# How many projection matmuls stand ahead of two blocks of a hybrid attention and delta-rule kernel

## The chip, the cores and the metric

The kernel runs on one core of one Trainium2 chip. The metric is device time in microseconds (us). The time before is the median of three runs.

## The reference

One transformer block on 1024 tokens of width 1024, in float32. A conditioning vector gives shifts, scales and gates. The normed input goes through one wide projection into nine parts: q, k and v of eight attention heads, q, k, v and z of eight heads of a gated delta rule, and two small logits. The attention is a sum of three dilated windows, which comes down to one biased softmax over 1024 keys. The delta rule works in chunks; within a chunk it solves a unit triangular system, and between chunks it carries a state. Both results go through an output projection, and a gated feed-forward layer follows.

```python
proj = h @ w_in[l]
q_a, k_a, v_a, q_d, k_d, v_d, z_d, b_d, a_d = jnp.split(proj, split_points, axis=-1)
y_attn = _dilated_attention(...)            # 8 heads of 64
y_delta = _gated_deltanet(...)              # 8 heads of 64, chunks, triangular solve, scan over chunks
y = jnp.concatenate([y_attn, y_delta], axis=-1) @ w_out[l]
x = x + g1 * y
h = _rmsnorm(x, norm_ffn_g[l]) * (1.0 + sc2) + sh2
y = (jax.nn.silu(h @ w_gate[l]) * (h @ w_up[l])) @ w_down[l]
```

## The kernel before, in words

The eight delta heads go in two groups of four (`delta(0)`, `delta(1)`). For each group the kernel convolves and transposes k and q, forms the products within chunks of 128 tokens (`delta_prep`), and inverts the triangular matrices (`delta_inverse`). The inverse has two parts. The diagonal 32x32 blocks are inverted on VectorE by 31 rounds of two instructions (lines 862 and 866), written to a DRAM scratch (`tn_d`, line 869) and read back in another layout (`tn`, line 871). Then the levels join the blocks into 64 and 128 by small matmuls on TensorE (tiles `lv`, `lw`, `lx`, lines 894 to 931), with copies on ScalarE and VectorE between them; the four heads go through them interleaved, `SKEW` = 4 steps apart. After the levels `delta_scan` walks over the eight chunks in order (tiles `st`, `o`, `yt`).

The large projections that nobody needs at once are a stock. The generator `others()` yields them step by step, in this order: z of the first delta group, then k, q and v of the second, z of the second (`z1`), the attention values in two halves (`va`, tile `g_va`), and q and k of the four head pairs (tile `g_a`), k first. A step is three matmuls, since each operand is split into a high and a low part: 128 columns by 256 for z and values (`proj_t`, counted as 0.32), by 512 for the others (`proj_d`, counted as 0.64). The generator `mixed()` adds the modulation matmuls (`mods`) after every 1.9 counted units, except while `quiet[0]` is set.

Three things draw on the stock. `turn(name)` draws `FILL[name]` counted units and then orders the matmuls of its block behind the last drawn one. `hold(what, us)` draws until `what` is complete, then `us` more, and orders the first matmuls of the levels behind the last drawn one; its arguments come from `LEVELS`, one pair for each group. And `until(...)` and `run(...)` draw what is left at certain places: all of z, values and pair 0's q and k before the attention, and the rest after the first pair's attention.

```python
LEVELS = ("qd", 4), ("z1", 28)
...
with hold(*LEVELS[g]) if step == 0 else ExitStack():
...
with turn(f"S{h}_{qb}_{c0}"):       # scores of head h, query block qb, keys from c0
```

The numbers are lower bounds on the order, not the order itself: the scheduler sorts instructions by priority and by when it reckons them ready, and so it places more of the stock between dependent matmuls (in the levels, in the scan, ahead of the first score) than these numbers ask for. At run time each engine takes its queue in the order that this gives.

The attention (`attend`) starts with `att_load(0)`: the head's q and k come back from DRAM (`raw`, two buffers), ScalarE makes QS and KS of them, GpSimd the low part KL (line 1227), and `att_score` multiplies QS with KS (line 1252) and with KL (line 1253). Its first block is `S0_0_0`. The first transposes have `et0_0_0` (1.92) and the first value product `y0_0` (0.64) as draws of their own.

Of the kernel before, what the change touches and what calls it, by code (L numbers as in the profile page):

```python
# [27 lines left out]
TCB = 3  # L28
MODS = 1.9
EARLY = 1  # L30
LEVELS = ("qd", 4), ("z1", 28)
TAIL = 4
AHEADF = 2
XB, ETB, AT, AV = 5, 4, 1, 3
# [13 lines left out]
    "et7_5_4": 0.64,  # L48
    "et2_7_0": 0.64,
    "et7_7_0": 0.64,  # L50
    "S0_0_0": 3.84,
    "et0_0_0": 1.92,
    "sy1_6": 1.92,
    "kk1_3_0_k": 0.64,
# [15 lines left out]
def build(tc, I, out):  # L70
# [772 lines left out]
    def delta_inverse(g, st):  # L843
# [92 lines left out]
        for step in range(3 * SKEW + 8):  # L936
            if step % SKEW == 0 and step // SKEW < 4:
                heads.append(head(step // SKEW))
            with hold(*LEVELS[g]) if step == 0 else ExitStack():
                quiet[0] = True  # L940
# [195 lines left out]
    def hold(what, us):  # L1136

        until(lambda: what in done)
        while us > 0:
            us -= next(fill[0])  # L1140
        return tc.issue_after(last[0].ins)
# [740 lines left out]
```

## Time and profile before

| | |
|---|---|
| median of three runs | 1458.61 us (1457.56 to 1468.36) |
| span of the profiled execution | 1472.9 us, 24559 instructions |
| mean granted TensorE clock in it | 0.964 |
| busy: PE, DVE, ACT, POOL | 95%, 59%, 45%, 19% of the span |
| longest lines of the chain that ended last | feed-forward matmuls (line 1513) and down projection (line 1699) |

The span is that of one execution under the profiler, from its first to its last instruction; the page gives no other time for this execution. It is longer than any of the three timed runs. The times of the parts below are those of the profiled execution.

PE is TensorE, PEld its weight loads, DVE VectorE, ACT ScalarE, POOL GpSimd, SP the engine that issues the transfers. The granted clock of PE is given as a fraction of its full rate; in this execution it is 1.00 or 0.50, and it changes at multiples of 3.41 us.

### The profile page before, as it was taken

Reading aid. Unit: us, or ns where it says so; the run is one execution under the profiler, and the core shown is the slowest. Engines: PE = TensorE matmul, PEld = TensorE weight load, DVE = VectorE, ACT = ScalarE, POOL = GpSimd, SP = SyncE. Lnnn points to the kernel's source line nnn. Section 1 sums busy time; section 2 is a strip of 40 time slices with the busy share of each in tenths; the row PEclk is TensorE's granted clock in tenths of the full one; section 3 lists DMA queues with packets and bytes.
Section 4 is the critical chain, followed back from the end, with each engine's and each line's share of the span. In section 5 each row is a group of like instructions: output and inputs, shape, how many; then the busy total and the mean of one; then the engine's idle time right before and its main releaser. Section 6 shows DMA issues by size and latency. Waiting matters only on the chain.

```text
span 1472.9 us, 24559 instructions
## 1 busy us (share of the span) xinstructions
PE 1400.0 (95%) x8984; PEld 1140.2 (77%) x8984; DVE 872.2 (59%) x1676; ACT 667.2 (45%) x1279; POOL 287.0 (19%) x267
## 2 busy tenths in 40 slices
PE   7998999988999989999999979999999999999997
PEld 4777767877889868777777758888888888888886
DVE  3687843565733332276525896766666676565477
ACT  3488414248122244476526733333333333445446
POOL 1344512244302332544235000000000000000000
PEclk9998999899957999999999989999999999999999
DMA  8736573475511535743165534454444565866666
GB/s 306 247 108 173 151 221 113 134 218 147 170 46 44 154 104 142 203 129 116 51 220 187 158 122 142 164 160 161 152 157 152 158 217 178 277 206 209 196 219 236
DMA packets 171345, 244.64 MB, mean 166 GB/s; under 512 B 33014, under 2 KB 76327, under 8 KB 171224
## 3 DMA queue, kind: packets, MB, share of 16 engines
q1 hardware_dynamic: 171224, 243.07, 52.7%
q8 instruction: 71, 1.16, 0.3%
q14 instruction: 50, 0.41, 0.1%
HBM read 180.25 MB, written 67.48 MB: 168 GB/s over the span
## 4 chain that ended last, share of the span: by engine, by line
PE 62%; DVE 7%; DMA 5%; ACT 2%; issue 2%; POOL 1%; SPq 0%; ACTq 0%; DVEq 0%
PE wga L1513 8%; PE wua L1513 8%; PE X L1699 6%; PE g_a L567 5%; PE wuc L1513 4%; PE wgc L1513 4%; PE Z L1699 4%; PE wo L567 4%; PE y L1293 3%; PE tr L1276 2%; PE Y L1699 2%; PE g_va L590 2%; PE wub L1513 2%; PE wgb L1513 2%; PE S L1252 1%
## 5 line engine op out<-in xcount | busy, mean ns | idle before, releaser
L1503 DVE TENSOR_TENSOR wl_db<-wr_db,wh_db 128x512 fp32r<-128x512 f32 x77 | 53.2, 691 | 76.1 <-ACT wh_db L1502 75.7
L1502 ACT CAST wh_db<-wr_db 128x512 fp32r<-128x512 f32 x77 | 47.9, 622 | 98.3 <-PE X L1699 41.3
L1699 PE MATMUL X<-wl_db,wh_da 128*128 128x512 f32 x176 | 68.6, 390 | 0.1
L1699 PE MATMUL X<-wh_db,wl_da 128*128 128x512 f32 x176 | 68.5, 389 | 0.0
L1699 PE MATMUL X<-wh_db,wh_da 128*128 128x512 f32 x176 | 68.5, 389 | 0.0
L1263 POOL TENSOR_SCALAR X<-X,sc 128x128 f32<-128x128 f32 (+7 forms) x64 | 47.7, 750 | 67.7 <-DVE sc L1262 55.1
L1261 ACT ACTIVATE X<-X,sc 128x128 f32<-128x128 f32 (+7 forms) x64 | 49.5, 775 | 23.8 <-DVE sc L1256 18.1
L1256 DVE CUSTOM_DVE_ANT_0 X<-S,ng 128x512 f32<-128x512 f32 (+3 forms) x64 | 36.8, 586 | 33.8 <-PE S L1253 21.7
L1222 DVE SCALAR_TENSOR_TENSOR QS<-raw,QS 64x1024 fp32r<-64x1024 f32 x8 | 12.6, 1572 | 70.3 <-ACT QS L1221 70.3
L567 PE MATMUL wo<-yh,wh_wo 128*128 128x512 f32 x128 | 52.0, 408 | 2.1 <-DVE xo L1339 1.0
L1503 DVE TENSOR_TENSOR wl_da<-wr_da,wh_da 128x512 fp32r<-128x512 f32 x77 | 52.6, 685 | 1.2 <-ACT wh_da L1502 1.2
L567 PE MATMUL g_a<-hh,wh_a 128*128 128x512 f32 x128 | 50.6, 395 | 0.0
L567 PE MATMUL g_a<-hh,wl_a 128*128 128x512 f32 x128 | 50.5, 395 | 0.0
L567 PE MATMUL wo<-yh,wl_wo 128*128 128x512 f32 x128 | 50.5, 396 | 0.0
L567 PE MATMUL g_a<-hl,wh_a 128*128 128x512 f32 x128 | 50.2, 392 | 0.0
L567 PE MATMUL wo<-yl,wh_wo 128*128 128x512 f32 x128 | 50.2, 394 | 0.0
L1502 ACT CAST wh_da<-wr_da 128x512 fp32r<-128x512 f32 x77 | 47.3, 616 | 5.8 <-PE wua L1513 5.8
L1293 PE MATMUL y<-et,va 128*64 128x128 f32 x576 | 46.0, 280 | 1.8 <-ACT et L1281 1.8
L1502 ACT CAST wh_wg_s<-wg_s 128x512 fp32r<-128x512 f32 x33 | 20.5, 622 | 58.0 <-PE wuc L1513 22.6
L1276 PE MATMUL tr<-ident,X 128*128 128x128 f32 x288 | 44.5, 280 | 2.2 <-ACT et L1281 2.0
L216 POOL TENSOR_TENSOR wl_wo<-wr_wo,wh_wo 128x512 fp32r<-128x512 f32 x24 | 32.8, 1366 | 57.4 <-ACT wh_wo L215 50.7
L1293 PEld LDWEIGHTS y<-et,va 128*64 128x64 f32 x576 | 33.7, 136 | 12.8 <-issue 8.7
(530 smaller groups left out, 4429.8 us busy)
## 6 DMA issues: line engine op xcount, KB each, us to landing
wr_da<-ao_d SPq DMA_DIRECT2D x77, 256.0 KB, 2.9
wm<-in_wada SPq DMA_DIRECT2D x64, 256.0 KB, 3.5
wr_wg<-in_wg SPq DMA_DIRECT2D x48, 256.0 KB, 3.0
wr_wu<-in_wu SPq DMA_DIRECT2D x48, 256.0 KB, 2.7
ao_d<-a SPq DMA_DIRECT2D x44, 256.0 KB, 2.2
wr_wd<-in_wdn SPq DMA_DIRECT2D x44, 256.0 KB, 3.1
wr_db<-wt_d SPq DMA_DIRECT2D x44, 256.0 KB, 2.7
ao_d<-as SPq DMA_DIRECT2D x33, 256.0 KB, 2.0
```

The source lines that it names most:

```text
L216: (eng or nc.gpsimd).tensor_tensor(out=lo[:, :n], in0=raw[:, :n], in1=hi[:, :n].bitcast(F32), op=ALU.subtract)
L567: last[0] = nc.tensor.matmul(ps, a[:, w0], b[k0 + k4][:, cs], start=(i == 0), stop=(i == n - 1))
L590: last[0] = nc.tensor.matmul(ps[:, :n], a[k][:, ts_], b[:, w0], start=(i == 0), stop=(i == 23))
L1256: nc.vector.tensor_tensor_reduce(out=X[:, c0:c1], in0=ps[:, 0 : c1 - c0], in1=ng[:, u + c0 : u + c1], scale=1.0, scalar=(3e38 if m is None ...
L1261: nc.scalar.activation(X[:, 0:nk], X[:, 0:nk], AF.Exp, scale=-1.0, bias=m, accum_out=sc[:, 2:3])
L1263: nc.gpsimd.tensor_scalar(out=X[:, 0:nk], in0=X[:, 0:nk], scalar1=sc[:, 3:4], scalar2=0.0, op0=ALU.mult, op1=ALU.add)
L1276: nc.tensor.transpose(ps[:, (kb - c0) * P : (kb - c0 + 1) * P], X[:, kb * P : kb * P + P], ident)
L1293: nc.tensor.matmul(yps[64 * e : 64 * e + 64, yc], va[:, kb, 64 * e : 64 * e + 64], ets[e][:, kb, :], start=(kb == 0), stop=(kb == qb),)
L1502: nc.scalar.copy(hi, src)
L1503: (eng or nc.vector).tensor_tensor(out=lo, in0=src, in1=hi.bitcast(F32), op=ALU.subtract)
L1513: nc.tensor.matmul(ps, a[:, w0], b, start=(first and k == 0 and n_ == 0), stop=(k == 3 and n_ == 2), skip_group_check=True,)
L1699: nc.tensor.matmul(bank[b], a[:, ts_], w, start=(first and f == 0 and n_ == 0), stop=(f == NF - 1 and n_ == 2), skip_group_check=True,)
```

## The change

Two numbers change. The second group's levels start after 36 counted units of value projections instead of 28, and the first attention score after 14.08 counted units of q and k projections instead of 3.84. The work itself is the same; the later draws find less of the stock left.

```diff
-LEVELS = ("qd", 4), ("z1", 28)
+LEVELS = ("qd", 4), ("z1", 36)
...
-    "S0_0_0": 3.84,
+    "S0_0_0": 14.08,
```

## The prediction

> **What bounds the kernel now.** I read the page first: who is busy, the granted clock by slice, the chain.
>
> ```profile
> PE 1400.0 (95%) x8984; PEld 1140.2 (77%) x8984; DVE 872.2 (59%) x1676; ACT 667.2 (45%) x1279; POOL 287.0 (19%) x267
> PEclk9998999899957999999999989999999999999999
> PE 62%; DVE 7%; DMA 5%; ACT 2%; issue 2%; POOL 1%; SPq 0%; ACTq 0%; DVEq 0%
> ```
>
> PE is busy nearly all the time and carries 62% of the chain. The projections are a fixed stock of matmuls that PE works off around the delta rule; moving some of them changes no sum of work. So a move pays only where PE stands idle, or where its clock changes. The clock line points at one place: the two slices from 405 to 479 us show 5 and 7 tenths. I cut that region, and two others with a falling clock, into windows of 3.41 us, the step in which the clock changes in this trace (columns: window, its length, PE busy with count, granted clock, DMA share, GB/s).
>
> ```profile
> 263.84:267.26 3.42, 2.05 (x17) 1.00 0.93 301
> 267.26:270.67 3.41, 3.41 (x18) 0.50 0.68 224
> ...
> 403.79:407.20 3.41, 3.41 (x31) 1.00 0.85 272
> 407.20:410.62 3.42, 0.75 (x7) 1.00 1.09 190
> 410.62:414.03 3.41, 3.06 (x69) 0.50 0.13 44
> ...
> 458.40:461.82 3.42, 3.42 (x19) 0.50 0.00 0
> 461.82:465.23 3.41, 3.41 (x32) 1.00 0.03 8
> ...
> 472.06:475.47 3.41, 2.21 (x19) 1.00 0.27 77
> ...
> 530.08:533.50 3.42, 1.92 (x9) 1.00 0.91 235
> 533.50:536.91 3.41, 1.66 (x7) 1.00 0.27 83
> 536.91:540.32 3.41, 2.21 (x7) 0.50 0.18 61
> ```
>
> After a window with 0.75, 1.66 or 2.05 us of busy time the clock is halved; after one with 1.92 or 2.21 it is not, so the limit is near 2 of 3.41 us, and depends on what ran. From 410.62 to 461.82 the clock stays halved for 15 windows though PE is busy. What emptied the window before it is in the timeline of PE:
>
> ```profile
> 407.67 0.28 PE L590 MATMUL g_va<-wh_va,hh 128*128 128x256 f32 x1
> 410.96 1.92 PE L894 MATMUL lv<-tn,dt 32*32 32x32 f32 x64 [3.01 <-DMA tn<-tn_d]
> ```
>
> The stock that the code orders ahead of group 2's levels runs out at 407.95; the levels wait for the inverse of the diagonal blocks on its way through DRAM. That is 3.0 us of idle PE, and then the half clock. Last, the region by stages (length, busy time with count of PE, PEld, DVE, ACT, POOL, clock, DMA, GB/s): levels of group 1; gap; levels of group 2; scan at half and at full clock; pure projections to the end of head pair 0; projections of pair 1 ahead of the first score; start of attention; rest of pair 0; the remaining projections.
>
> ```profile
> 236.03:261.79 25.76, 25.76 (x502) 19.13 (x502) 14.82 (x27) 10.49 (x24) 5.68 (x6) 1.00 0.28 82
> 407.96:410.96 3.00, 0.00 (x0) 0.00 (x0) 0.00 (x0) 0.18 (x2) 0.00 (x0) 0.94 1.21 233
> 410.96:452.76 41.80, 41.80 (x520) 37.66 (x520) 13.14 (x28) 10.31 (x26) 3.18 (x4) 0.50 0.04 12
> 452.76:461.82 9.06, 9.06 (x44) 9.06 (x43) 2.46 (x11) 1.75 (x5) 1.62 (x2) 0.50 0.00 0
> 461.82:496.43 34.61, 32.19 (x248) 29.74 (x247) 23.30 (x78) 11.36 (x33) 16.68 (x18) 1.00 0.33 92
> 496.43:515.30 18.87, 18.87 (x84) 15.64 (x85) 0.00 (x0) 5.29 (x13) 5.16 (x4) 1.00 0.67 204
> 515.30:526.85 11.55, 11.55 (x52) 9.53 (x51) 1.22 (x1) 3.89 (x6) 3.02 (x2) 1.00 0.64 167
> 526.85:541.90 15.05, 9.26 (x37) 6.87 (x36) 4.03 (x17) 6.70 (x16) 6.01 (x6) 0.83 0.44 131
> 541.90:571.20 29.30, 28.78 (x248) 22.22 (x247) 15.90 (x56) 18.29 (x40) 10.72 (x13) 0.97 0.15 46
> 571.20:619.90 48.70, 48.70 (x218) 40.28 (x218) 4.12 (x7) 17.46 (x33) 20.05 (x13) 1.00 0.74 196
> ```
>
> The two level stages have nearly the same instructions (502 and 520). Group 1, entered with no gap, took 25.76 us at full clock; group 2, entered after the gap, 41.80 at half. So one dense start decides a whole stage: at full clock the small matmuls of the levels did not lose it, at half clock they did not win it back.
>
> **The change, part by part.** It adds and removes no instruction; two numbers decide after how much of the stock a block may start.
>
> *Levels, 28 to 36.* A step of a value projection is three matmuls counted as 0.32. So 88 steps become 113: 25 steps, 75 matmuls, are ordered ahead of the levels of group 2. Their price is read from PE rows for the value projections and for q and k:
>
> ```profile
> 397.80:407.90 10.10, 10.04 (x82) 1.00 0.66 190
> 571.20:619.90 48.70, 47.91 (x210) 1.00 0.74 196
> ```
>
> 10.04/82 = 0.122 us each for a value projection, 47.91/210 = 0.228 for q and k. 75 of them take 9.2 us: PE runs from 407.95 to 417.1 with no gap, and the levels start at 417.1 instead of 410.96, 6.1 us late. What goes with them: three evacuations on ACT and three stores on SP. The evacuation just before already waited for its store:
>
> ```profile
> ACT va L1058 <- DMA va_d<-va: 3.4, 1, 3.4
> 406.68 3.38 SPq L1059 DMA_DIRECT2D va_d<-va  x2
> ```
>
> Between evacuations now lie 24 x 0.122 = 2.9 us, the DMA share falls from 1.21 in the gap to 0.04 in the levels, and nothing on SP but these stores stands behind the inverse's load, which is issued before them. I take their cost as 0; without that cover one store's 3.4 us of waiting would stand in the fill, and it is the upper bound.
>
> The late start itself I also cost at 0. Behind the scan PE has 18.87 us of pure projections before the q and k of pair 0 are complete; taking 9.2 from them leaves 9.7. PE still ends this stretch, not the delta chain. Without that cover the cost would be 6.1 us.
>
> What it wins. The gap: 3.0. The levels at full clock: 41.80 - 25.76 = 16.0. The first of the scan, 9.06 us at half clock: the readout's four matmuls took 0.95 us there and 0.56 later,
>
> ```profile
> 457.18 0.95 PE L1008 MATMUL o<-VN,qk 128*128 128x64 f32 x4
> 466.37 0.56 PE L1008 MATMUL o<-VN,qk 128*128 128x64 f32 x4
> ```
>
> so 9.06 x (1 - 0.56/0.95) = 3.7. Sum 22.7. Bounds: if the delta chain's other engines hold it and the clock wins nothing, 3.0; if all 51.2 us at half clock ran twice as fast, 3.0 + 25.6 = 28.6. I take 22.7, since group 1's levels are a direct sample of the same code at full clock.
>
> [...]
>
> *First score, 3.84 to 14.08.* A step of a q or k projection counts 0.64: 6 steps become 22. One step more is taken by the loop that completes pair 0, so 69 matmuls must precede the first score. The scheduler already placed 52 there (row 515.30). The score moves back by 17 x 0.228 = 3.9 us. PE at the start of attention:
>
> ```profile
> 526.89 0.39 PE L1252 MATMUL S<-KS,QS 128*128 128x128 f32 x2
> 529.32 0.50 PE L1253 MATMUL S<-KL,QS 128*128 128x128 f32 x2 [1.34 <-POOL KL L1227]
> 533.76 0.43 PE L1293 MATMUL y<-et,va 128*64 128x128 f32 x2 [1.76 <-ACT et L1281]
> 535.66 0.50 PE L1252 MATMUL S<-KS,QS 128*128 128x128 f32 x2 [1.47 <-ACT KS L1226]
> 538.11 0.80 PE L1253 MATMUL S<-KL,QS 128*128 128x128 f32 x2 [1.22 <-POOL KL L1227]
> ```
>
> With 69 ahead the first score starts at 515.30 + 69 x 0.228 = 531.0, past 529.3, when KL of the first head is there: the first wait goes. The second half of the first score is then 1.7 us late, and transposes and values of that head behind it; but the second head's KL comes at 538.1, by loads that PE does not touch, so this is covered. The waits add to 5.8 us. Asked for ahead of the first value product are now 1 + 22 + 3 + 1 = 27 steps, 81 matmuls; 72 were run before the 210 of the last row. So 9 x 0.228 = 2.0 us of work moves into waits. Bounds: 1.7 lost if the late first head counts in full, 5.8 won if all waits fill. I take 2.0. The half clock at 536.91 I leave, since waits of about 3.8 remain.
>
> **Sum.** 22.7 + 2.0 = 24.7 us; everything after 571 follows PE and shifts. The profiled span goes from 1472.9 to 1448.2. That span is 14.3 us above the median of the timed runs, 1458.61 (1457.56 to 1468.36); I know no other time of that execution, what lies around its span included. If the timed runs contain the same half clock, the time is 1458.6 - 24.7 = 1434 us.
>
> **Rivals.**
>
> *The timed runs mostly lack the long half clock.* For it: the profiled span is 14.3 us longer than the median and one timed run is 10 us longer than the others, sizes that a stretch worth about 20 us can explain. Against: a gap of 3.0 us leaves at least 1.5 us idle in one of two windows wherever they lie, and the work behind it is 32x32 matmuls. Then only gap and waits remain: 3.0 + 2.0 = 5.0, and 1453.6 us. If one window of half clock went with it, another 3.41 x (1 - 25.76/41.80) = 1.3: 1452.3. [...]
>
> *The clock falls in the scan instead.* The scan has waits (window 472.06 was busy 2.21, near the limit), and group 1's scan lost the clock at 267.26. If it then stays halved to the scan's end, the 32.19 us of PE work in row 461.82 grow by 0.95/0.56 - 1 = 0.70, 22.4, of which its 2.4 idle us absorb part: +20.0, and the net win is 4.7: 1453.9. Against: in group 1 it lasted three windows, and the q and k matmuls that now fall into the scan are twice as long as the value matmuls they replace.
>
> *Slower: the half clock moves into the first attention pair.* The score's late start gathers the remaining waits just ahead of the dense part; if the halved clock then holds through it as it held through the levels, the 29.30 us of row 541.90 grow by 41.80/25.76 - 1 = 0.62, 18.2. In an execution that never lost the clock in the levels this is 18.2 - 3.0 = +15.2: 1473.8 us. It decides once a window ahead of 541.9 is busy under about 2 us and the next ones do not win the clock back. Against: here the clock came back after two windows, by 543.7.
>
> **How the numbers follow.** Forecast 0.56; long half clock absent 0.24; clock lost in the scan 0.10; lost in attention 0.10. A per cent, 14.6 us, is about what a measurement of this kernel can tell from no change. The forecast is faster by 1.7%: 0.56. The two middle cases are within 1%: 0.34. The last is slower: 0.10. The forecast's own range is 1428 to 1441 (bounds 28.6 + 2.0 won; 22.7 - 3.4 - 1.7 won). The range of 8 in 10 goes from 1428 to 1457: it takes in the middle cases and leaves out the last.
>
> **What would show it.** Right: no wait of PE for the inverse's load; clock 1.00 through the levels of group 2 and these near 26 us; first `st` near 443; q and k of pair 0 complete near 493; 69 or more `g_a` matmuls ahead of the first score and no wait of it for KL. Wrong: a gap ahead of the levels still there, levels near 42 us at 0.50 even without a gap, a scan that grows by what the levels lose, or attention at 0.50 beyond two windows.

## The result and the profile after

The changed kernel takes 1456.07 us, the median of 20 runs (1450.73 to 1460.81). The kernel before, in 20 runs beside them, takes 1461.08 us (1453.81 to 1486.69). The ratio is 0.9954 with a 95% interval of 0.9934 to 0.9973: by it 6.7 us less (5.0 between the medians), where 24.7 were forecast. The measured median lies above the forecast's own range, which ended at 1441, and just inside the wider one to 1457, which had been drawn to take in two rivals. The ratio leaves out executions over 1.5% above the fastest of their kernel, two of the kernel before and none after; here they are part of what the change does. Over all executions the means are 1464.1 and 1455.7 us, and eight of the twenty before, but none after, take over 1464 us.

The profiled executions are 1472.9 and 1457.5 us long, 15.4 us apart. The page after, busy time and granted clock by slice:

```profile
PE 1381.9 (95%) x8984; PEld 1121.6 (77%) x8984; DVE 872.7 (60%) x1676; ACT 668.8 (46%) x1279; POOL 284.5 (20%) x267
PEclk9998999998999989999999989999999999999999
```

The 5 and 7 in the clock line are gone, and PE is busy 18 us less for the same matmuls. In windows of 3.41 us (length, PE busy and count, clock, DMA share, GB/s) the place ahead of the levels now reads:

```profile
409.32:412.73 3.41, 3.41 (x31) 1.00 1.06 187
412.73:416.15 3.42, 1.96 (x17) 1.00 0.15 51
416.15:419.56 3.41, 3.33 (x27) 1.00 0.22 77
419.56:422.97 3.41, 3.41 (x125) 1.00 0.13 43
```

The clock stays at 1.00 into the levels. One thing is left in the second row. The timeline of PE and the chain show what:

```profile
416.23 0.39 PE L590 MATMUL g_va<-wh_va,hh 128*128 128x256 f32 x1 [1.55 <-ACT va L1058]
420.02 1.20 PE L894 MATMUL lv<-tn,dt 32*32 32x32 f32 x64
```

```profile
414.97 0.40 ACT tc L900
415.38 0.41 ACT tc L901
415.81 0.38 ACT va L1058
```

An evacuation of the values (the copy that empties a PSUM bank, `va` in line 1058) stood in ACT's queue behind six of the levels' own copies (`tc`), which had waited 3.0 us for the inverse's load and ran from 413.30 to 415.79; so the projections waited 1.55 us for their bank. The stages after (length; PE, PEld, DVE, ACT, POOL; clock; DMA share; GB/s): levels, scan, projections, start of attention in two pieces, attention of pair 0, remaining projections.

```profile
420.09:443.97 23.88, 23.88 (x505) 20.27 (x504) 11.39 (x24) 10.12 (x23) 8.14 (x8) 1.00 0.21 63
443.97:483.46 39.49, 36.89 (x271) 33.44 (x272) 26.07 (x88) 12.53 (x38) 15.98 (x18) 1.00 0.23 65
483.46:502.80 19.34, 19.34 (x87) 15.98 (x86) 0.00 (x0) 4.12 (x10) 3.85 (x3) 1.00 0.77 225
502.80:518.50 15.70, 8.41 (x35) 6.13 (x34) 2.91 (x5) 7.04 (x10) 6.91 (x5) 0.78 0.53 157
518.50:522.00 3.50, 3.46 (x10) 2.87 (x11) 1.39 (x9) 2.28 (x10) 1.33 (x3) 0.51 0.11 37
522.00:552.30 30.30, 29.59 (x258) 22.73 (x257) 16.86 (x60) 18.51 (x40) 10.19 (x12) 1.00 0.16 49
552.30:597.50 45.20, 45.20 (x201) 37.42 (x201) 3.66 (x3) 17.33 (x32) 17.52 (x12) 1.00 0.77 210
```

The levels take 23.88 us instead of 41.80. The start of attention did not improve:

```profile
508.29 0.39 PE L1252 MATMUL S<-KS,QS 128*128 128x128 f32 x2
510.50 0.50 PE L1253 MATMUL S<-KL,QS 128*128 128x128 f32 x2 [1.36 <-POOL KL L1227]
516.12 0.79 PE L1252 MATMUL S<-KS,QS 128*128 128x128 f32 x2 [4.88 <-ACT KS L1226]
518.54 0.80 PE L1253 MATMUL S<-KL,QS 128*128 128x128 f32 x2 [1.09 <-POOL KL L1227]
```

These waits are 7.3 us together; before they were 5.8 with the one for `et`. The first wait for KL, which the change was to fill, is still 1.36. The last of the stock's matmuls starts at 599.1 us, where before it was 618.7. Of these 19.6 us the spans show 15.4: what follows takes 853 to 859 us in the thirteen profiles of this document, 854.2 before and 858.4 after.

So in one pair of profiles the mechanism of the forecast appears nearly as written, and yet the median moves by about a quarter of what was forecast. Theory A: the long half clock comes only in some executions of the kernel before. Theory B: every execution has it, and the changed kernel gives most of the gain back later.

### The profile page after: what moved, and what is told of

It reads as the page before. It is cut to its first block, busy times and chain, and to the rows that moved or that the text cites. A ratio compares the mean times of both kernels' runs of the same rounds, so it can differ in the third digit from the quotient of the medians.

```text
span 1457.5 us, 24558 instructions
## 1 busy us (share of the span) xinstructions
PE 1381.9 (95%) x8984; PEld 1121.6 (77%) x8984; DVE 872.7 (60%) x1676; ACT 668.8 (46%) x1279; POOL 284.5 (20%) x267
## 4 chain that ended last, share of the span: by engine, by line
PE 63%; DVE 6%; DMA 4%; ACT 3%; issue 2%; POOL 1%; SPq 0%; ACTq 0%; DVEq 0%; POOLq 0%
PE wga L1513 8%; PE wua L1513 8%; PE X L1699 6%; PE g_a L567 5%; PE wuc L1513 4%; PE wgc L1513 4%; PE Z L1699 4%; PE wo L567 4%; PE g_va L590 3%; PE y L1293 3%; PE tr L1276 2%; PE Y L1699 2%; PE wub L1513 2%; PE wgb L1513 2%; PE S L1252 1%
## 5 line engine op out<-in xcount | busy, mean ns | idle before, releaser
L1261 ACT ACTIVATE X<-X,sc 128x128 f32<-128x128 f32 (+7 forms) x64 | 49.6, 776 | 22.4 <-DVE sc L1256 17.2
L1502 ACT CAST wh_wg<-wr_wg 128x512 fp32r<-128x512 f32 x33 | 20.4, 622 | 51.4 <-issue 20.0
```

Source lines behind the costliest of these rows:

```text
L1261: nc.scalar.activation(X[:, 0:nk], X[:, 0:nk], AF.Exp, scale=-1.0, bias=m, accum_out=sc[:, 2:3])
L1502: nc.scalar.copy(hi, src)
```

## The experiments

In these runs the kernel before ran alongside again, with medians of 1461.58 (35 runs), 1469.3 (35 runs) and 1464.37 us (16 runs).

**The kernel before once more** (no edit).

> The kernel before, unchanged, to see how its executions differ. Theory A (the half clock ahead of the levels comes only in some executions): another profiled execution can show the levels of group 2 near 24 to 26 us at clock 1.00, and the times spread over 10 us or more, longer ones at a lower mean clock. Theory B (every execution has it, and the changed kernel gives most of the gain back later): again about 15 windows at 0.50 from the gap on, levels near 41.8 us, mean clock near 0.964.

Median 1460.79 us of 12 (1449.26 to 1479.61), ratio 0.9994 (0.9958 to 1.0029). The profiled execution took 1479.61 and had the 15 half windows again. The times spread over 30 us, and each execution has a mean clock: 1449.26 at 0.982, 1460.35 at 0.975, 1470.02 at 0.967, 1479.61 at 0.959. A straight line through the 216 timed executions told of here whose clock is on record gives 1.25 us for each 0.001 of clock. The spread speaks for A; the profile alone could not tell.

**Only the levels.**

```diff
-LEVELS = ("qd", 4), ("z1", 28)
+LEVELS = ("qd", 4), ("z1", 36)
```

> Only the levels' number goes from 28 to 36; the first score keeps 3.84. Theory A: no gap, levels near 24 us at clock 1.00 in the profile, and a ratio to before of 0.995 to 0.998 (3.0 us of gap plus the rarer slow executions). Theory B: the ratio is the same as with the whole change only if the loss lies outside the first score; if the later first score is what gives it back, this version alone is faster than the whole change by 5 us or more (ratio 0.985 to 0.99).

Median 1455.36 us of 12, ratio 0.9964 (0.9933 to 0.9995), none over 1463.6. In its profile there is no gap, and the levels take 23.8 us at clock 1.00. This is the whole effect of the change as far as it can be measured; it is not the later first score that makes the change fall short of the forecast.

**Only the first score.**

```diff
-    "S0_0_0": 3.84,
+    "S0_0_0": 14.08,
```

> Only the first score's number goes from 3.84 to 14.08; the levels keep 28. By the prediction: 2.0 us won. By the two traces read after the result (8 or 9 matmuls more ahead of the first score, waits at the start of attention 7.3 us against 5.8): between 1 us lost and 1 us won, ratio 0.999 to 1.001, under either theory.

Ratio 1.0000 (0.9965 to 1.0035), six of 12 over 1464. The interval is 5 us wide to either side, so the times can't tell 2.0 us from nothing; the trace can. The stretch from pair 0's end to the end of its attention, and in it the first score of the second head:

```profile
497.20:556.70 59.50, 52.72 (x347) 0.91 0.33 93
519.50 0.80 PE L1252 MATMUL S<-KS,QS 128*128 128x128 f32 x2 [5.18 <-ACT KS L1226]
```

Here the first score did not wait for KL at all, as the prediction had it. But the wait for the second head's KS grew from 1.47 to 5.18 us, and the stretch takes 59.5 us; in the kernel before it is 57.9 and 58.0 (rows further down).

The profile brought more. It has a gap ahead of the levels like the kernel before (3.62 us), but only two half windows from it on, and a span of 1456.7. The same code so far, a gap of the same kind, and another course of the clock: A.

**Fewer steps ahead of the levels.**

```diff
-LEVELS = ("qd", 4), ("z1", 28)
+LEVELS = ("qd", 4), ("z1", 20)
```

> The levels' number goes down from 28 to 20, so that 25 steps less stand ahead of the levels and PE idles about 12 us there, which fills two whole clock windows wherever they lie. Theory A: now every execution has the half clock through the levels, which the fast executions of before lack: gap 9.2 us longer and some 16 to 20 us of slower levels and scan, 20 to 29 us over before (ratio 1.014 to 1.02). Theory B: before has the half clock anyway, so only the longer gap is added: 9.2 us (ratio 1.006) or less.

This did not do what it was to do: the gap stayed at 3.6 us. PE's waits:

```profile
PE lv L894 <- DMA tn<-tn_d: 3.6, 1, 3.6
```

The scheduler puts 276 value matmuls ahead of the levels with 20, and 274 with 28, so these numbers hardly bound, and whether a longer gap costs more stays untested. With 36 it is 342: the change moved 68 matmuls there and not 75. Ratio 1.0017 (0.9973 to 1.0061), median of all 12 1472.79 us, eight over 1464: as the kernel before, within such spreads.

**Two more executions of the kernel before** (no edit).

> The kernel before, unchanged, one more look, for an execution that recovers early. Theory A: either 15 half windows and a first dense window behind the gap with under 2.5 us of value matmuls, or 2 to 3 half windows and one with over 2.55 us.

> The same again: by theory A the first window at half clock that holds over about 2.55 us of value matmuls is the last one at half clock, and the stretch from the first value matmul to the end of pair 0's projections is 20 us shorter in an execution that recovers than in one that does not.

The first took 1461.2 us, the second 1479.1. Stages of PE in the first, in the second and in the changed kernel, all from the first value matmul: to the levels, the levels, to the end of pair 0's projections, to the end of pair 0's attention.

```profile
366.60:411.90 45.30, 40.39 (x374) 0.99 0.60 175
411.90:438.50 26.60, 26.60 (x520) 0.90 0.05 18
438.50:495.80 57.30, 54.68 (x365) 1.00 0.39 118
495.80:553.70 57.90, 51.88 (x344) 0.94 0.35 96
```

```profile
366.00:411.00 45.00, 40.34 (x372) 1.00 0.62 176
411.00:452.80 41.80, 41.77 (x519) 0.50 0.03 12
452.80:513.30 60.50, 58.10 (x364) 0.93 0.36 112
513.30:571.30 58.00, 51.72 (x344) 0.94 0.34 96
```

```profile
367.60:420.00 52.40, 48.68 (x440) 1.00 0.55 156
420.00:443.90 23.90, 23.90 (x504) 1.00 0.21 63
443.90:492.70 48.80, 46.20 (x314) 1.00 0.32 92
492.70:552.30 59.60, 51.56 (x347) 0.91 0.36 109
```

The sums are 187.1, 205.3 and 184.7 us. Against the second execution the change wins 20.6; against the first only 2.4: 4.1 in the first three stages, less 1.7 in the last. If the eight of twenty executions over 1464 us are of the kind of the second, 0.4 x 20.6 + 0.6 x 2.4 = 9.7 us would be the mean gain; the means of the twenty runs each differ by 8.4. That they are is an estimate: of the kernels with the gap, four profiled executions over 1464 us had the 15 half windows and three under it had one or two, but none between 1462 and 1474 was profiled.

What goes with the early return of the clock is seen in the value matmuls of each window. First execution, then second, then the profile before, `b_again`, `score_only` and `levels20`; each row gives the value matmuls alone (tile `g_va`) in the second window at half clock:

```profile
413.96:417.37 3.41, 2.92 (x13) 0.50 0.00 0
...
414.05:417.46 3.41, 2.48 (x12) 0.50 0.00 0
...
414.03:417.44 3.41, 2.48 (x12) 0.50 0.02 5
...
415.77:419.18 3.41, 2.48 (x12) 0.50 0.00 0
...
415.58:418.99 3.41, 2.62 (x13) 0.50 0.00 0
...
413.62:417.04 3.42, 2.49 (x12) 0.50 0.11 38
```

Behind the first product of the levels stands a piece of 13 value matmuls, the densest in the whole stage; in the profile before it runs from 412.81 to 415.95. In the first execution it lies whole in one window (2.92 us of value matmuls), in `score_only` all but its first 0.5 us does (2.62), and that window is the last at half clock. In the other four the edge of a window cuts it, and the second window holds its later part and the first matmuls of the next piece (2.48, 2.49 us). There the clock comes back only 13 windows later, in the scan; none of the windows between holds more than 2.1 us of value matmuls. In the two that recovered, the half clock began 1.04 and 1.34 us ahead of the levels, in the others 0.3 to 0.4. So in these six profiles it goes with the place of the windows whether an execution takes about 18 us more (1479.1 against 1461.2 us in the two extra executions). That place differed between executions of the same code, and the next run tests the reading by an edit. A busy PE was not enough to bring the clock back: in the profile before it was busy for all of each of 14 windows in a row at half clock, with 0.00 to 2.48 us of value matmuls in a window.

**A dense piece in the levels.** This leaves the gap and lengthens the dense piece behind the first product of the levels.

```diff
-    "S0_0_0": 3.84,
+    "S0_0_0": 3.84, "lb1_0": 4.48,
```

> The kernel before with one more draw: 4.48 counted units (14 steps) of value projections ahead of the second small product of the levels (lb1_0 4.48), so that about 38 value matmuls stand in one block behind the first product. The gap of 3.0 to 3.6 us stays. Theory A with its mechanism (the gap halves the clock every time; only a window with about 2.55 us or more of 128x256 matmuls brings it back, and in the levels of the kernel before only the first dense piece can hold that, depending on where the windows lie): the half clock ends after 2 or 3 windows in every execution, no time over about 1464 us, and the times look like those of levels_only plus 2 to 4 us. Rival (the gap itself, its idle time, is what costs; or the clock is lost for another reason): long half clock in the profile again or times over 1470 us in a third of the runs, as before.

Median 1456.59 us of 12 (1450.50 to 1465.21), ratio 0.9942 (0.9907 to 0.9978); one of 12 over 1464, at 1465.2, where the kernel before had 19 of 35. In its profile the gap is 3.6 us, and the first window at half clock is full of value matmuls and is the only one (rows of `g_va` alone):

```profile
409.93:413.35 3.42, 3.42 (x18) 0.50 0.01 2
413.35:416.76 3.41, 2.43 (x20) 1.00 0.11 38
```

So most of the cost lies in the clock that does not return, and not in the gap. The twelve times carry this more than the one profile, since the first execution above came back early without such a block.

**Levels at 32.**

```diff
-LEVELS = ("qd", 4), ("z1", 28)
+LEVELS = ("qd", 4), ("z1", 32)
```

> Only the levels' number, at 32 instead of 36 (100 steps instead of 113, about 1.5 us of projections beyond the gap instead of 6). If closing the gap is all that counts: no gap, no long half clock, no time over about 1464 us, a median within 2 us of levels_only (1455.4). If the 8 units win for another reason than the gap: half of the win.

Median 1455.71 us of 12, ratio 0.9933 (0.9898 to 0.9968), no gap in the profile. But, against what was expected, two executions took 1472.63 and 1477.75 at clocks of 0.965 and 0.964. With so small a margin the long half clock still seems to come at times; no profile caught one, so that stays open.

**Levels at 44.**

```diff
-LEVELS = ("qd", 4), ("z1", 28)
+LEVELS = ("qd", 4), ("z1", 44)
```

> Only the levels' number, at 44: 25 steps more than 36, so that the levels start another 9 us late with the gap long closed. The prediction costed the late start at nothing as long as pure projections stand behind the scan; with 44 hardly any are left (18.9 us less 18 to 19). By that: within 2 us of levels_only (1455.4). If the late start costs in full: up to 9 us more.

Median 1460.91 us of 12 (1456.37 to 1466.45), ratio 0.9959 (0.9925 to 0.9994). To pair 0's end it is as fast as with 36:

```profile
371.40:432.10 60.70, 57.84 (x500) 1.00 0.51 149
432.10:456.80 24.70, 24.70 (x485) 1.00 0.21 61
456.80:496.90 40.10, 37.39 (x273) 1.00 0.22 65
496.90:557.00 60.10, 51.36 (x340) 0.91 0.44 125
```

The first three sum to 125.5; in the changed kernel it is 125.1. In these profiles the late start costs nothing. The times do not confirm it: the median is 5.5 us above `levels_only`, between the two expectations, while the ratios to the kernel before, run beside each of them, are alike (0.9959 and 0.9964). In the one profile 2.8 us of the difference lie ahead of these stages, where the code is the same: the first value matmul starts at 371.4 instead of 368.6 us. The mean clock of the whole execution is 0.972 instead of 0.975; what held this one up ahead of its first value matmul stays open.

**A draw ahead of the second head's score**, on top of the changed kernel.

```diff
-    "S0_0_0": 14.08,
+    "S0_0_0": 14.08, "S1_0_0": 5.12,
```

> The changed kernel with one more draw: 5.12 units (8 steps, 24 matmuls, 5.4 us) of q and k projections ahead of the first score of the second head (S1_0_0 5.12). In the changed kernel PE waits 4.9 us there for KS, and 3 windows go at half clock. If that wait is what the later first score failed to fill: the wait gone or under 1 us, fewer half windows, 3 to 6 us won over the changed kernel (median near 1451, ratio to before near 0.992). If the head is late by as much as is put in: no change.

Median 1457.96 us of 12, ratio 0.9935 (0.9901 to 0.9969), by the times not to be told from the changed kernel; 1451 was hoped for. The wait for KS is gone, but another of the same length stands in its place, by PE's waits:

```profile
PE g_a L567 <- ACT sp_a L1067: 5.3, 1, 5.3
PE S L1253 <- POOL KL L1227: 1.3, 1, 1.3
```

Now a projection waits for its bank, whose evacuation stands in ACT's queue (519.48 us) behind QS and KS of the second head, and these wait for their loads (QS 0.38 us up to 515.63, KS 1.85 us up to 518.53). The matmuls put into this wait helped only as far as their evacuations could pass: 5.3 us of waiting stand where 4.9 stood.

**A candidate.**

```diff
-LEVELS = ("qd", 4), ("z1", 28)
+LEVELS = ("qd", 4), ("z1", 32)
...
-    "S0_0_0": 3.84,
+    "S0_0_0": 3.84, "lb1_0": 2.56,
```

> Candidate: levels at 32 and lb1_0 at 2.56 (8 steps ahead of the second small product), first score at 3.84 as before. By theory A no gap and no long half clock, and the order at the first attention score stays that of the kernel before (60 matmuls of pair 1 ahead of it, 57 us from pair 0's end to the end of the first attention pair instead of 59.6): median 1453 to 1455, no time over 1464.

Median 1454.93 us of 12 (1450.52 to 1460.01), ratio 0.9941 (0.9913 to 0.9968), none over 1464. The same four stages as above:

```profile
373.10:418.10 45.00, 43.78 (x403) 1.00 0.60 176
418.10:444.60 26.50, 25.69 (x531) 1.00 0.14 42
444.60:496.50 51.90, 49.28 (x326) 1.00 0.36 107
496.50:554.30 57.80, 52.22 (x344) 0.94 0.37 106
```

They sum to 181.2 us, against 184.7 for the changed kernel. Its times beat the kernel before; against the changed kernel the 1.1 us between medians of runs at different times show nothing.

## Why the prediction was wrong, step by step

*The step that failed* is the one from the profiled span to the timed runs: "if the timed runs contain the same half clock". With the 1.8 us that lie between span and time in the changed kernel (1457.5 and 1459.26), the profiled execution before would be one of 1474.7 us; of 120 timed executions of this kernel 99 were faster. The prediction took 22.7 us, a gain that only such an execution has to give, from a median that mostly consists of others. The runs showed two kinds of execution in its place: by the estimate above about four of ten had 20.6 us to give up to the end of pair 0's attention, the others 2.4. The span 14.3 us above the median was the sign, and the first rival took it so, at 1453.6 us, with 0.24. It named the outcome best; the chance was too small.

*Its argument against that rival was half right.* After a gap of 3.0 to 3.7 us the clock was at half in every profile that has the gap (seven of seven). But I took it from one execution that a lost clock stays lost through the levels. In three of the seven it came back after one or two windows, according to how much of the dense piece fell into one window.

*Levels and scan, 22.7 us.* Right for an execution with the long half clock: from the first value matmul to the end of pair 0's projections it was 147.3 us in the second of the two extra executions (45.0 + 41.8 + 60.5) and is 125.1 now (52.4 + 23.9 + 48.8), 22.2 less. For the other kind, the first execution, it is 129.2 - 125.1 = 4.1, near the rival's 3.0 plus 1.3 for a window.

*Evacuations at nothing.* Off by 1.55 us: I looked at the stores and not at what stands ahead of the evacuation in ACT's queue.

*Late start at nothing.* Right, by the stages of the changed kernel and of 44, as far as one profile of each can show it.

*First score, 2.0 us won.* Wrong in sign: from pair 0's end to the end of its attention it takes 59.6 us, before 57.9 and 58.0. I set the end of pair 0's projections at 515.3; the 96th of its matmuls ended at 513.4, so 60 stood ahead of the score, not 52, and the change added 9, not 17. Up to the last stage 78 of pair 1's matmuls had run before and 81 after, so that 3 moved into waits, 0.7 us, and not 9. And these did not fill the waits. Ahead of the second head's first score stand 72 of them before, after and in `score_only` alike: the nine that now stand ahead of the first score used to stand behind it. The second head's score begins 22.4 us after pair 0's end before, 22.3 in `score_only` and 23.4 after, whatever stands in between, since its KS waits for loads (ACT idles 0.86 us for them before and 1.80 us after, ahead of KS at 534.57 and 515.02); so what was moved forward left a longer wait there, 5.18 and 4.88 us instead of 1.47.

In the changed kernel, though not in `score_only`, the loads of the first head also came apart: a weight load stands between them in SP's queue. Before, then after:

```profile
518.68 2.39 SPq L1215 DMA_DIRECT2D raw<-qk_d  x4
```

```profile
498.80 1.75 SPq L1215 DMA_DIRECT2D raw<-qk_d  x3
502.84 0.34 SPq L214 DMA_DIRECT2D wr_a<-in_wd  x1
503.22 0.45 SPq L1215 DMA_DIRECT2D raw<-qk_d  x1
```

The fourth load is issued 2.7 us behind the third's end, after the weight load, and the first product with KL starts 17.8 us after pair 0's end instead of 16.0; so the first wait stayed. `levels_only` has the same order of loads, 68 matmuls ahead of the first score though its draw is 3.84, and takes 59.8 us. So each of the two numbers alone brings this cost, in one profile each, and together they bring it once.

*The other rivals.* In the profile after, the clock did not fall in the scan (1.00 in the row from 443.97), and in attention it came back after three windows (half from 511.72 to 521.96 us).

## What to carry to other kernels

Before a stage of small matmuls, look not only at whether PE idles, but whether it could win back its clock in that stage: here a dense block brought the ratio to 0.9942 with the gap of 3.6 us still there (`dense`). One profile is one execution; when its span lies off the median of the timed runs, compare its clock with theirs, and profile others before a term is taken from it. A number that orders work is a bound: compare what the trace has there with what the number asks for. And matmuls moved ahead of a wait fill nothing if they used to stand ahead of it already: count those between the last wait and the next.

## What the runs showed of the hardware that I had not expected

The same program, with a gap of 3.5 and of 3.7 us, ran 18 us apart (1479.1 and 1461.2), and the difference goes with where the clock's windows of 3.41 us lay: the half clock began 0.39 and 1.34 us ahead of the levels. A PE busy for all of a window at half clock stayed there with 2.49 us of 128x256 matmuls in it (`levels20`) and came back with 2.62 (`score_only`). Levels at full clock kept it with 1.0 to 2.0 us of projection matmuls in a window (1.24 to 1.96 in `score_only`, 1.00 in one of `dense`).
